# A hybrid RG-LRU and SSD layer on one core: seven weight subtractions, eight additions and the conv tails leave GpSimd, and the RG gate weights are issued first

## The chip, the cores and the metric

The kernel runs on one core of one Trainium2 chip. Its time is the device time of that core in microseconds. The matrix unit is called PE (weight loads: PEld), VectorE is DVE, ScalarE is ACT, GpSimd is POOL and SyncE is SP. PE shows two granted clocks in the records, 1.2 and 2.4 GHz, written 0.50 and 1.00; a stretch over which it changes shows a value between.

## The reference

One layer of a decoder trunk on T = 544 tokens: a prompt of 512 and eight samples of 4 tokens, width 1024, in fp32.

```
x = x + 0.5 * post1(SwiGLU1(pre1(x)))
x = x + postM(Mixer(preM(x)))
x = x + 0.5 * post2(SwiGLU2(pre2(x)))

proj = u @ w_in          # -> rg_x, rg_g, z, xbc, dt_raw, g_rg, g_ssd
rg_xc = causal_conv(rg_x)                     # 4 taps
gate_a = sigmoid(blockwise rg_xc @ wa + ba)   # 8 blocks of 128 x 128
gate_x = sigmoid(blockwise rg_xc @ wx + bx)
a = exp(-8 gate_a softplus(-lam));  h = scan(a, rg_xc gate_x sqrt(1 - a^2))
y_rg = h * gelu(rg_g)
xs, B, C = split(silu(causal_conv(xbc)))
y_ssd = rmsnorm_by_group((ssd_scan(xs, softplus(dt), A, B, C) + ssd_d * xs) * silu(z))
out = (sigmoid(g_rg) * (y_rg @ Wr) + sigmoid(g_ssd) * (y_ssd @ Ws)) @ w_out
```

It also returns the last state of both scans and the last three rows ahead of each convolution (the conv states), for the prompt and for every sample.

## The kernel before, in words

Activations lie transposed, features on the 128 partitions and the 544 tokens along the row, in two halves of 272. Every weight is fetched in raw tiles of up to 1024 x 256 by DMAs of SP (line 54; two tiles, so at most one is fetched ahead of the one in use). The class `Weights` cuts it into blocks of 1024 x 128 and splits each in two: ACT casts it to a high part `wh` (line 68), and a subtraction gives the low part `wl` (line 69). That subtraction is VectorE's, except in seven blocks, where the spec's flag `low` is set and the block's number is odd: there it is POOL's (line 61). Four blocks of `wh` and `wl` are kept, three of them ahead of use. A product is three matmuls for each 128 of depth and each half: high by high, low by high, high by low.

The work goes FFN1, mixer, FFN2. In the mixer, the first products (`first_products`, line 653) run dt and the first columns of the RG branch and fill tiles of the normalised activations; then come pairs of RG blocks, each with a background generator `rg_steps` (line 800): convolution (`conv`, four taps of VectorE at line 757), gate weights fetched and split (lines 806 to 812), gate products (line 830), the scan on VectorE (line 869) and the gelu product. Blocks (2, 3) and (0, 1) are first; a loop (line 1194) does (4, 5) and (6, 7). `dt_steps` (line 703) makes softplus, cumulated decays and their transposes (PE line 739) in the middle of that. Then eight SSD groups follow: convolution of B, C and x, chunked scan, gating, square (ACT line 1138), the sum of two squares (line 1141) and a matmul with ones (line 1146) for the group's norm. Behind them come the two output projections, the merge and FFN2.

`conv_last` (line 765) keeps the last three rows of each stretch of a convolution's input `cb` in a small tile `cq`, 9 stretches by 3 rows; it is called 40 times, with two POOL copies each time, the second after the first; PE transposes `cq` at line 776 for the conv states. `ssd_d` is fetched (lines 699 to 701) by two DMAs, each of 64 partitions by 16 elements that lie two elements apart in memory.

PE's order is written by hand (`tc.manual_schedule`, line 97): the products of the main path call `ptick` after each matmul, and every few matmuls one step of the oldest background generator is issued among them. The other engines' order is a scheduler's. POOL's DMAs share one queue (q0), SP's another (q1).

Of the kernel before, what the change touches and what calls it, by code (L numbers as in the profile page):

```python
# [9 lines left out]
F32 = mybir.dt.float32  # L10
# [8 lines left out]
P = 128  # L19
D = 1024  # L20
KD = 8
LP = 512
NB = 8
# [11 lines left out]
class Weights:  # L35
    def __init__(self, nc, pool, specs, ahead):
        self.nc = nc
        self.pool = pool
        self.specs = specs
        self.ahead = ahead  # L40
        self.blocks = [(s, o) for s, (ap, kt, cols, low) in enumerate(specs) for o in range(0, cols, P)]
        self.raw = {}
        self.done = {}
        self.n_raw = 0
        self.n_blk = 0
        self.pos = 0

    def _load(self):
        s = self.n_raw
        if s >= len(self.specs):  # L50
            return
        ap, kt, cols, low = self.specs[s]
        t = self.pool.tile([P, 8, 2 * P], F32, tag="wraw", name="wraw", bufs=WRAW)
        self.nc.sync.dma_start(t[:, :kt, :cols], ap.rearrange("(k p) c -> p k c", p=P))
        self.raw[s] = t
        self.n_raw += 1

    def _split(self):
        nc = self.nc
        s, o = self.blocks[self.n_blk]  # L60
        sub = nc.gpsimd if self.specs[s][3] and self.n_blk % 2 else nc.vector
        while self.n_raw <= min(s + WRAW - 1, len(self.specs) - 1):
            self._load()
        kt = self.specs[s][1]
        src = self.raw[s][:, :kt, o:o + P]
        h = self.pool.tile([P, 8, P], F32R, tag="wh", name="wh", bufs=WBLK)
        l = self.pool.tile([P, 8, P], F32R, tag="wl", name="wl", bufs=WBLK)
        nc.scalar.copy(h[:, :kt], src)  # L68
        sub.tensor_sub(l[:, :kt], src, h[:, :kt].bitcast(F32))  # L69
        self.done[self.n_blk] = (h, l)  # L70
        self.n_blk += 1

# [13 lines left out]
def hybrid_layer_kernel(  # L86
# [9 lines left out]
    nc = tc.nc  # L96
    ctx.enter_context(tc.manual_schedule(engines={mybir.EngineType.PE}))
    V, S, G, PE = nc.vector, nc.scalar, nc.gpsimd, nc.tensor
    dma = nc.gpsimd.dma_start
# [20 lines left out]
    FCH = (6, 8, 8)  # L120
    FC0 = (0, 6, 14)
# [5 lines left out]
    def end_order(kind, c):  # L127

        return [(kind, (c, n), 0) for n in range(4)] + [("post", 0, 0)] + [(kind, (c, n), 1) for n in SECOND] + [("post", 1, 1)]

    def ffn_order():

        order = [("gu", 0, 0), ("gu", 1, 0), ("gu", 1, 1), ("gu", 0, 1), ("gu", 2, None)]
        for c in range(3):
            if c:
                order += [("gu", p, None) for p in range(FC0[c] // 2 + 1, (FC0[c] + FCH[c]) // 2)]
            if c < 2:
                order += [("gu", FC0[c + 1] // 2, None)]
                order += [("wd", (c, n), None) for n in range(4)]
        return order + end_order("wd", 2)  # L140

    def ffn_specs(wg, wu, wd):
        sp = []
        for kind, i, h in ffn_order():
            if kind == "gu" and (i, h) != (1, 1):
                cs = slice(256 * i, 256 * i + 256)
                sp += [(wg[0, :, cs], 8, 256, False), (wu[0, :, cs], 8, 256, False)]
            elif kind == "wd" and not (h == 1 and i[1] in KEPT):
                c, n = i
                sp.append((wd[0, P * FC0[c]:P * (FC0[c] + FCH[c]), 256 * n:256 * n + 256], FCH[c], 256, False))  # L150
        return sp

    def win_spec(c0, n, low=False):
        return [(w_in[0, :, c0 + o:c0 + min(o + 256, n)], 8, min(256, n - o), low) for o in range(0, n, 256)]

    specs = ffn_specs(ffn1_wg, ffn1_wu, ffn1_wd)
    specs += win_spec(8192, 128)
# [5 lines left out]
    GATES_RG, GATES_SSD = ((0,), (1, 2), (3,)), ((), (4,), (), (5,), (), (6,), (), (7,))  # L163

    def gate_specs(qs):
        return [win_spec(8224 + 256 * q, 256, q < 3)[0] for q in qs]

    specs += gate_specs(GATES_RG[0])
    for i, r in enumerate(range(4, 8, 2)):
        specs += win_spec(128 * r, 256, True) + win_spec(1024 + 128 * r, 256, True) + gate_specs(GATES_RG[i + 1])  # L170
    for g in range(8):
        specs += win_spec(6144 + 128 * g, 128) + win_spec(7168 + 128 * g, 128) + win_spec(4096 + 256 * g, 256)
        a, b = gate_specs(GATES_SSD[g]), win_spec(2048 + 256 * g, 256)
        specs += b + a if g == 7 else a + b
    specs += [(w_proj_rg[0, :, 256 * q:256 * q + 256], 8, 256, False) for q in range(4)]
    for i in range(2):
        specs += [(w_proj_ssd[0, 1024 * i:1024 * i + 1024, 256 * q:256 * q + 256], 8, 256, False) for q in range(4)]
    for kind, i, h in end_order("out", 0):
        if kind == "out" and not (h == 1 and i[1] in KEPT):
            specs.append((w_out[0, :, 256 * i[1]:256 * i[1] + 256], 8, 256, False))  # L180
    specs += ffn_specs(ffn2_wg, ffn2_wu, ffn2_wd)
    W = Weights(nc, wpool, specs, WBLK - 1)

# [48 lines left out]
    def split(h, l, src):  # L232
        S.copy(h, src)
        V.tensor_sub(l, src, h.bitcast(F32))

    def wait(n):
        for _ in range(n):
            yield
# [432 lines left out]
    def mt(shape, tag, bufs, dt=F32):  # L671
        return pm.tile(shape, dt, tag=tag, name=tag, bufs=bufs)
# [7 lines left out]
    def t_b(shape, dt=F32):  # L680
        return mt(shape, "big", 12, dt)

    def t_s(shape, dt=F32):
        return mt(shape, "small", 14, dt)

    hfin = pm.tile([P, KD, 9], F32, name="hfin")
    tokT = pm.tile([P, 3, 4, 32], F32, name="tokT")
    toks = pm.tile([96, 3, 32], F32, name="toks")
    Es = pm.tile([P, 16, TS], F32, name="Es")
    Dc = pm.tile([P, 16], F32, name="Dc")  # L690
# [5 lines left out]
    dtc = pm.tile([32, 4], F32, name="dtc")  # L696
    dma(dtc[:, 0:1], ssd_dt_bias.rearrange("o h -> h o"))
    dma(dtc[:, 1:2], ssd_a_log.rearrange("o h -> h o"))
    for h2 in range(2):
        src = ssd_d.rearrange("o (q h) -> o h q", h=2)[0, h2:h2 + 1, :]  # L700
        dma(Dc[64 * h2:64 * h2 + 64, :], src.to_broadcast([64, 16]))

    def dt_steps(dt_):

# [48 lines left out]
    def conv(buf, ws, b):  # L753
        o = t_cv()
        S.activation(o[:, :CO], buf[:, 0:CO], AF.Identity, scale=ws[0], bias=b)  # L755
        for k in range(1, 4):
            V.scalar_tensor_tensor(o[:, :CO], buf[:, k:k + CO], ws[k], o[:, :CO], op0=ALU.mult, op1=ALU.add)  # L757
        ahead["cb"] -= 1
        return o
# [5 lines left out]
    def conv_last(buf):  # L765

        q = mt([P, 9, 3], "cq", 8)
        G.tensor_copy(q[:, 0:8], buf[:, LP:LP + 56].rearrange("p (b u) -> p b u", b=NB)[:, :, 0:3])
        G.tensor_copy(q[:, 8], buf[:, LP + 56:LP + 59])
        return q  # L770

    def conv_state(o_p, o_s, qs, f, df):
# [27 lines left out]
    def rg_steps(r0, bufs, gsb):  # L800
        qs = [lasts.pop(0) for _ in range(2)]
        rs = (r0, r0 + 1)
        col = lambda r, i: pT[:, r, i:i + 1]
        xcs, chs, wqs, gas, gxs, avs = [], [], [], [], [], []
        for r in rs:
            wr = t_s([P, 2, P])
            dma(wr[:, 0], rg_wa[0, r])
            dma(wr[:, 1], rg_wx[0, r])
            wq = [t_s([P, 2, P], F32R) for i in range(2)]
            split(wq[0], wq[1], wr)  # L810
            wqs.append(wq)
            xc = conv(bufs[r - r0], [col(r, R_RGW + i) for i in range(4)], col(r, R_RGB))
            ch = t_b([P, CB], F32R)
            cl = t_b([P, CB], F32R)
            split(ch[:, :CO], cl[:, :CO], xc[:, :CO])
            xcs.append(xc)
            chs.append((ch, cl))
            yield from wait(4)
# [95 lines left out]
    def group_steps(g, tiles):  # L914
# [73 lines left out]
        def fin():  # L988
            St = st8["S"]
            fs = ps_tile()  # L990
            for p in range(2):
                PE.transpose(fs[:, P * p:P * p + P], St[:, 2 * p:2 * p + 2].rearrange("p h d -> p (h d)"), ident)
            fo = t_s([P, 2, P])
            S.copy(fo, fs[:, :256].rearrange("p (a n) -> p a n", a=2))
            dma(o_p_ssd[0, 0, h4].rearrange("(a h) d n -> (h d) a n", a=2), fo)
# [133 lines left out]
        sqs = []  # L1129
        for p in range(2):  # L1130
# [6 lines left out]
            q = t_b([P, T])  # L1137
            S.activation(q, y, AF.Square, scale=0.5)
            ys.append(y)
            sqs.append(q)  # L1140
        G.tensor_add(sqs[0], sqs[0], sqs[1])
        fin()
        yield from wait(12)
        v = py_tile()
# [2 lines left out]
        r = sqs[1]  # L1147
# [11 lines left out]
    def rg_inputs(r):  # L1159
        bufs = []  # L1160
        for j in range(2):
            acc = unit(KD, xh, xl)
            bufs.append(rg_buf(r + j))
            for h in range(2):
                conv_in(bufs[j], acc[:, h, :TH], h)
        return bufs
# [25 lines left out]
    gate_units(GATES_RG[0])  # L1192
    bg.append(dt_steps(dt_))
    for i, r in enumerate(range(4, KD, 2)):
        b = rg_inputs(r)
        bg.append(rg_steps(r, b, rg_gates(r)))
        gate_units(GATES_RG[i + 1])
    for g in range(8):
        out = {}
        for i, f in enumerate((16 + g, 24 + g, 2 * g, 2 * g + 1)):  # L1200
            acc = unit(KD, xh, xl)
            q, t = f // 8, f % 8
            buf = conv_buf(cst[:, t, :].rearrange("p (b w q) -> p b w q", b=NB, w=3)[:, :, :, q])
# [64 lines left out]
    for n in range(KD):  # L1268
# [5 lines left out]
        h = mt([P, T], "mh", 8, F32R)  # L1274
        l = mt([P, T], "ml", 8, F32R)
# [98 lines left out]
```

## Time and profile before

| | |
|---|---|
| median of 3 runs | 1775.37 us (1774.06 to 1775.75) |
| profiled execution | 1772.28 us |
| its span | 1770.5 us |
| mean granted clock | 0.987 |
| PE busy | 1689.6 us (95%) |
| DVE busy | 1002.2 us (57%) |
| ACT busy | 730.4 us (41%) |
| POOL busy | 328.3 us (19%) |

The busy shares are averages over stages: FFN1 ends near 460 us of the span, the RG blocks lie between 460 and 680, the SSD groups between 680 and 1140, and projections and FFN2 fill the rest. PE is busy nearly always, so what can move the time is the sum of the short stretches in which PE waits, and those in which its granted clock is 0.50. POOL works only between about 440 and 1170 us.

### The profile page before, as it was taken

The numbers are of one execution on the slowest core, as the hardware profiler recorded it, in microseconds if no ns is written. First come the engines' busy times: TensorE is split into PE (matmuls) and PEld (weight loads), VectorE is DVE, ScalarE is ACT, GpSimd is POOL, SyncE is SP. The second block draws the span as 40 slices with busy tenths as digits, with TensorE's granted clock in tenths as the row PEclk, the third lists the DMA queues.
The fourth block names the chain that finished last, engine by engine and source line by source line (L and its number), as shares of the span: only waits on it lengthen the run. The fifth ranks groups of instructions, "written<-read, shape, count | busy, mean of one in ns | idle before, by whom it ended". The sixth has DMA issues, their size and how long they took to land. (4 is left out here: it accounts for less than half of the span.)

```text
span 1770.5 us, 31999 instructions
## 1 busy us (share of the span) xinstructions
PE 1689.6 (95%) x13419; PEld 1642.0 (93%) x13419; DVE 1002.2 (57%) x1728; ACT 730.4 (41%) x1145; POOL 328.3 (19%) x475
## 2 busy tenths in 40 slices
PE   7999999999989898998999999999999999999997
PEld 6999999999989897988988988899998999999996
DVE  5432333347556678788798687776557532233336
ACT  6322221234367585545445445433346323221232
POOL 0000000001143325355355445241000000000000
PEclk9999999999989899999999999999999999999998
DMA  6313323323742334433433544665424323223231
GB/s 199 108 54 114 96 72 96 96 96 104 113 147 91 113 107 123 143 114 102 142 116 113 149 127 131 204 192 192 176 95 138 100 69 119 81 87 96 85 107 51
DMA packets 204541, 206.17 MB, mean 116 GB/s; under 512 B 10493, under 2 KB 190777, under 8 KB 204142
## 3 DMA queue, kind: packets, MB, share of 16 engines
q1 hardware_dynamic: 196030, 179.61, 32.7%
q0 software_dynamic: 8368, 24.53, 5.0%
q8 instruction: 105, 1.72, 0.4%
q14 instruction: 38, 0.31, 0.1%
HBM read 178.42 MB, written 25.69 MB: 115 GB/s over the span
## 5 line engine op out<-in xcount | busy, mean ns | idle before, releaser
L68 ACT CAST wh<-wraw 128x1024 fp32r<-128x1024 f32 (+1 forms) x274 | 283.4, 1036 | 632.6 <-PE acc L268 519.0
L268 PE MATMUL acc<-xh,wh 128*128 128x272 f32 x2576 | 543.7, 292 | 0.0
L268 PE MATMUL acc<-xh,wl 128*128 128x272 f32 x2576 | 541.0, 291 | 0.0
L268 PE MATMUL acc<-xl,wh 128*128 128x272 f32 x2576 | 538.8, 290 | 0.0
L69 DVE TENSOR_TENSOR wl<-wraw,wh 128x1024 fp32r<-128x1024 f32 (+1 forms) x267 | 324.7, 1218 | 319.4 <-ACT wh L68 316.2
L268 PEld LDWEIGHTS acc<-xh,wh 128*128 128x128 f32 x2576 | 408.3, 190 | 3.6 <-issue 1.4
L268 PEld LDWEIGHTS acc<-xl,wh 128*128 128x128 f32 x2576 | 407.9, 190 | 1.2 <-issue 0.4
L268 PEld LDWEIGHTS acc<-xh,wl 128*128 128x128 f32 x2576 | 406.6, 190 | 2.2 <-issue 0.8
L300 PE MATMUL acc<-xh,wh 128*128 128x272 f32 x384 | 114.0, 297 | 1.5 <-DVE xl L518 1.5
L300 PE MATMUL acc<-xh,wl 128*128 128x272 f32 x384 | 113.5, 296 | 0.0
L300 PE MATMUL acc<-xl,wh 128*128 128x272 f32 x384 | 113.0, 294 | 0.0
L427 POOL TENSOR_TENSOR xT<-xT,rt 128x272 f32<-128x272 f32 x4 | 3.5, 886 | 534.4 <-DVE rt L426 534.4
L361 DVE TENSOR_TENSOR gate<-gate,acc 128x544 f32<-128x544 f32 x36 | 26.0, 722 | 132.0 <-PE acc L268 132.0
L757 DVE SCALAR_TENSOR_TENSOR cv<-cb,hp,cv 128x568 f32<-128x568 f32 x96 | 89.5, 932 | 6.0 <-ACT cv L755 4.9
L268 PE MATMUL acc<-hh,wh 128*128 128x272 f32 x448 | 92.5, 288 | 0.0
L268 PE MATMUL acc<-hl,wh 128*128 128x272 f32 x448 | 92.2, 287 | 0.0
L268 PE MATMUL acc<-hh,wl 128*128 128x272 f32 x448 | 92.1, 287 | 0.0
L628 POOL MEMSET cb<- 128x3 f32 x40 | 4.1, 102 | 471.3 <-PE acc L300 432.8
L300 PEld LDWEIGHTS acc<-xh,wh 128*128 128x128 f32 x384 | 73.9, 192 | 2.2 <-DVE xl L518 1.6
L300 PE MATMUL acc<-hh,wh 128*128 128x272 f32 x256 | 75.1, 293 | 0.0
L300 PEld LDWEIGHTS acc<-xl,wh 128*128 128x128 f32 x384 | 74.0, 193 | 0.5
L300 PEld LDWEIGHTS acc<-xh,wl 128*128 128x128 f32 x384 | 73.8, 192 | 0.4
(351 smaller groups left out, 2698.4 us busy)
## 6 DMA issues: line engine op xcount, KB each, us to landing
wraw<-in_w_in_dram SPq DMA_DIRECT2D x34, 1024.0 KB
wraw<-in_ffn_wg_dram SPq DMA_DIRECT2D x24, 1024.0 KB
wraw<-in_ffn_wu_dram SPq DMA_DIRECT2D x24, 1024.0 KB
wraw<-in_ffn_wd_dram SPq DMA_DIRECT2D x20, 1024.0 KB
wraw<-in_w_in_dram SPq DMA_DIRECT2D x18, 512.0 KB
big<-acs_dram SPq DMA_DIRECT2D x32, 256.0 KB
big<-in_state_ssd_dram SPq DMA_DIRECT2D x32, 256.0 KB
out_dram<-big POOLq DMA_DIRECT2D x32, 256.0 KB, 3.3
```

The source lines that it names most:

```text
L68: nc.scalar.copy(h[:, :kt], src)
L69: sub.tensor_sub(l[:, :kt], src, h[:, :kt].bitcast(F32))
L268: PE.matmul(acc[:, h, :TH], w[:, k, :], r[k][:, HALF[h]], start=(k == 0 and i == 0), stop=(k == kt - 1 and i == 2))
L300: PE.matmul(acc[:, j, :TH], w[:, k, :], r[k][:, HALF[h]], start=(k == 0 and i == 0), stop=(k == kt - 1 and i == 2))
L361: V.tensor_mul(two(gs[j]), two(gs[j]), acc[:, :, :TH])
L427: (G if shared and k % 2 else V).tensor_add(xT[:, k, cs], xT[:, k, cs], t)
L628: G.memset(buf[:, 0:3], 0.0)
L757: V.scalar_tensor_tensor(o[:, :CO], buf[:, k:k + CO], ws[k], o[:, :CO], op0=ALU.mult, op1=ALU.add)
```

## The change

Five edits, in one kernel:

- the flag `low` goes, and all 274 subtractions of `wl` are VectorE's;
- the RG gate weights are fetched by a function `rg_weights`: eight DMAs for blocks 2, 3, 0 and 1 as soon as the mixer's pools are open, ahead of the memsets of `cz` and the DMAs of `dtc`; the eight for blocks 4 to 7 at the start of the loop's two turns, ahead of their inputs;
- `ssd_d` is fetched as one contiguous row of 32 to every partition (`Dr`), and two VectorE copies pick the elements out;
- `conv_last` is one ACT copy with an access pattern written by hand, of nine stretches of 3 rows, 7 elements apart;
- the sum of two squares in a group is VectorE's.

```diff
@@ class Weights, _split
-        sub = nc.gpsimd if self.specs[s][3] and self.n_blk % 2 else nc.vector
...
         nc.scalar.copy(h[:, :kt], src)
-        sub.tensor_sub(l[:, :kt], src, h[:, :kt].bitcast(F32))
+        nc.vector.tensor_sub(l[:, :kt], src, h[:, :kt].bitcast(F32))
@@ mixer, where its pools open
+    def rg_weights(rs):
+
+        for r in rs:
+            wr = t_s([P, 2, P])
+            dma(wr[:, 0], rg_wa[0, r])
+            dma(wr[:, 1], rg_wx[0, r])
+            wrs[r] = wr
+
+    wrs = {}
+    rg_weights((2, 3, 0, 1))
...
+    Dr = t_s([P, 16, 2])
+    dma(Dr.rearrange("p q h -> p (q h)"), ssd_d.to_broadcast([P, 32]))
     for h2 in range(2):
-        src = ssd_d.rearrange("o (q h) -> o h q", h=2)[0, h2:h2 + 1, :]
-        dma(Dc[64 * h2:64 * h2 + 64, :], src.to_broadcast([64, 16]))
+        V.tensor_copy(Dc[64 * h2:64 * h2 + 64, :], Dr[64 * h2:64 * h2 + 64, :, h2])
@@ conv_last
         q = mt([P, 9, 3], "cq", 8)
-        G.tensor_copy(q[:, 0:8], buf[:, LP:LP + 56].rearrange("p (b u) -> p b u", b=NB)[:, :, 0:3])
-        G.tensor_copy(q[:, 8], buf[:, LP + 56:LP + 59])
+        a = buf[:, LP:LP + 1]
+        S.copy(q, bass.AP(a.tensor, a.offset, [list(a.ap[0]), [7, 9], [1, 3]]))
@@ rg_steps
-            wr = t_s([P, 2, P])
-            dma(wr[:, 0], rg_wa[0, r])
-            dma(wr[:, 1], rg_wx[0, r])
+            wr = wrs.pop(r)
@@ group_steps
-        G.tensor_add(sqs[0], sqs[0], sqs[1])
+        V.tensor_add(sqs[0], sqs[0], sqs[1])
@@ loop over r = 4, 6
+        rg_weights((r, r + 1))
         b = rg_inputs(r)
```

Line numbers after the change differ: the subtraction is line 68, the gate weights' DMAs lines 689 and 690, the scan 877, the conv taps 767, the sum of squares 1149. PE's order of instructions is the same in both kernels. POOL has 384 instructions in its order instead of 479, DVE 1311 rows instead of 1292, and ACT 40 more copies.

Where the mixer opens, POOL's order before, from the write of the residual to DRAM (`xs_dram`) to the first three pairs of gate weights:

```order
L603 DMA xs_dram_112<-xT_157 128x4352
L695 MEMSET cz0_4781 128x256
L695 MEMSET cz1_4782 128x256
L697 DMA dtc_4785<-in_ssd_dt_bias_dram 32x1
L698 DMA dtc_4785<-in_ssd_a_log_dram 32x1
L701 DMA Dc_4778<-in_ssd_d_dram 64x16x1 x2
L807 DMA small_5085<-in_rg_wa_dram 128x128
L808 DMA small_5085<-in_rg_wx_dram 128x128
L807 DMA small_5117<-in_rg_wa_dram 128x128
L808 DMA small_5117<-in_rg_wx_dram 128x128
L807 DMA small_5462<-in_rg_wa_dram 128x128
L808 DMA small_5462<-in_rg_wx_dram 128x128
```

The same place after the change, right behind the write of the residual:

```order
L689 DMA small_4774<-in_rg_wa_dram 128x128
L690 DMA small_4774<-in_rg_wx_dram 128x128
L689 DMA small_4777<-in_rg_wa_dram 128x128
L690 DMA small_4777<-in_rg_wx_dram 128x128
L689 DMA small_4780<-in_rg_wa_dram 128x128
L690 DMA small_4780<-in_rg_wx_dram 128x128
L689 DMA small_4783<-in_rg_wa_dram 128x128
L690 DMA small_4783<-in_rg_wx_dram 128x128
L704 MEMSET cz0_4793 128x256
L704 MEMSET cz1_4794 128x256
L706 DMA dtc_4797<-in_ssd_dt_bias_dram 32x1
L707 DMA dtc_4797<-in_ssd_a_log_dram 32x1
```

The gate weights stood behind the two memsets and four other DMAs, two of them those of `ssd_d`; now all eight of the first blocks stand ahead of them. The fetch of `ssd_d` is the next row, and the eight DMAs for blocks 4 to 7 follow it.

On VectorE, at the scans of the first pair of RG blocks (`big` and `in` are tiles of the RG steps, `cv` is a convolution's result, `cb` its input), the order before:

```order
L757 SCALAR_TENSOR_TENSOR cv<-cb,pT,cv 128x568 x2
L860 MEMSET in 128x1 x2
L757 SCALAR_TENSOR_TENSOR cv<-cb,pT,cv 128x568
L861 TENSOR_TENSOR in<-in 128x568 x2
L867 COPY in<-pT 128x8 x2
L869 SCALAR_TENSOR_TENSOR big<-big,in 128x568 x2
L870 COPY hfin<-big 128x9
L873 SCALAR_TENSOR_TENSOR big<-z,big 128x512
L874 SCALAR_TENSOR_TENSOR big<-z,big 128x32
```

and after, from the first scan to the second split of the next pair's convolution (line 233, which was line 234):

```order
L877 SCALAR_TENSOR_TENSOR big<-big,in 128x568
L875 COPY in<-pT 128x8
L68 TENSOR_TENSOR wl<-wraw,wh 128x1024
L878 COPY hfin<-big 128x9
L881 SCALAR_TENSOR_TENSOR big<-z,big 128x512
L882 SCALAR_TENSOR_TENSOR big<-z,big 128x32
L877 SCALAR_TENSOR_TENSOR big<-big,in 128x568
L788 COPY cs<-ps 27x256
L878 COPY hfin<-big 128x9
L881 SCALAR_TENSOR_TENSOR big<-z,big 128x512
L882 SCALAR_TENSOR_TENSOR big<-z,big 128x32
L233 TENSOR_TENSOR big<-cv,big 128x568
```

The three conv taps that stood ahead of the scans stand behind both splits of line 233 now; a weight subtraction that was POOL's stands between the scans, and the copy of `cs`, which was behind the first split of line 234, is ahead of it.

On VectorE in `dt_steps`, whose results PE transposes, the order before:

```order
L713 TENSOR_TENSOR big<-big 32x544
L714 SCALAR_TENSOR_TENSOR big<-big 32x544
L724 TENSOR_SCALAR big<-big,dtc 32x544
L744 COPY small<-big 32x96
L725 SCALAR_TENSOR_TENSOR big<-big 32x544
L730 TENSOR_TENSOR big<-big 32x512
L730 TENSOR_TENSOR big<-big 32x32
```

and after:

```order
L723 TENSOR_TENSOR big<-big 32x544
L724 SCALAR_TENSOR_TENSOR big<-big 32x544
L734 TENSOR_SCALAR big<-big,dtc 32x544
L754 COPY small<-big 32x96
L735 SCALAR_TENSOR_TENSOR big<-big 32x544
L68 TENSOR_TENSOR wl<-wraw,wh 128x1024
L740 TENSOR_TENSOR big<-big 32x512
L740 TENSOR_TENSOR big<-big 32x32
```

A weight subtraction has come between the second and the third result that PE transposes there.

## Rows read from the trace of the kernel before

**Rows 1.** Waits of PE: engine, line, waited for: us in total, times, longest.

```profile
PE py L300 <- ACT wh L68: 8.5, 1, 8.5
...
PE ps L776 <- POOL cq L769: 4.9, 1, 4.9
...
PE py L830 <- DVE big L234: 3.9, 2, 2.7
...
PE py L1146 <- POOL big L1141: 2.3, 1, 2.3
...
PE py L830 <- ACT in L832: 1.6, 1, 1.6
```

**Rows 2.** Windows: us, busy of PE, PEld, DVE, ACT, POOL, PEclk, DMA share, GB/s.

```profile
480.00:490.00 10.00, 3.79 (x31) 3.56 (x29) 0.00 (x0) 0.00 (x0) 0.00 (x0) 0.88 0.80 29
483.70:497.90 14.20, 5.31 (x22) 4.90 (x22) 6.10 (x8) 6.05 (x12) 2.68 (x4) 0.64 0.32 101
500.00:505.60 5.60, 5.60 (x47) 5.60 (x47) 5.09 (x8) 4.60 (x9) 1.13 (x4) 1.00 0.74 232
548.20:555.90 7.70, 4.97 (x27) 4.92 (x27) 7.19 (x14) 3.20 (x4) 2.44 (x6) 0.78 0.57 199
587.60:600.30 12.70, 8.13 (x43) 7.54 (x42) 10.67 (x19) 4.58 (x9) 4.17 (x9) 0.60 0.44 110
667.30:675.40 8.10, 3.25 (x16) 3.21 (x16) 6.69 (x14) 2.79 (x5) 7.22 (x8) 0.79 0.79 226
...
1137.30:1143.00 5.70, 3.36 (x11) 2.83 (x11) 2.40 (x3) 1.05 (x2) 2.35 (x1) 0.70 0.82 268
```

**Rows 3.** Timeline of ACT: start, us, instruction, idle before and its releaser.

```profile
490.84 0.40 ACT L233 CAST small<-small 128x256 fp32r<-128x256 f32 x1 [18.36 <-DMA small<-in_rg_wx_dram]
```

**Rows 4.** Timeline of POOL, the fetch of `ssd_d`.

```profile
467.22 1.67 POOL L701 DMA_DIRECT2D Dc<-in_ssd_d_dram  x2
```

**Rows 5.** Line 701's own view: landing of its two DMAs.

```profile
DMA to landing us min/median/max: 14.2/18.2/22.3
```

**Rows 6.** Line 698's own view: landing of `ssd_a_log`, issued just before.

```profile
DMA to landing us min/median/max: 3.6/3.6/3.6
```

**Rows 7.** Line 808's own view: its issues, and landing of eight DMAs of gate weights.

```profile
L808 POOL DMA_DIRECT2D small<-in_rg_wx_dram x8: 547/547/558, 469.5 to 610.3; - x8
...
DMA to landing us min/median/max: 2.1/3.9/21.3
```

**Rows 8.** Timeline of DVE, at the first scans and in `dt_steps`.

```profile
540.00 1.65 DVE L757 SCALAR_TENSOR_TENSOR cv<-cb,pT,cv 128x568 f32<-128x568 f32 x2
...
543.98 4.75 DVE L869 TENSOR_TENSOR_SCAN big<-big,in 128x568 f32<-128x568 f32 x2
...
585.67 2.73 DVE L713 TENSOR_TENSOR big<-big 32x544 f32<-32x544 f32 x1
...
635.18 1.33 DVE L869 TENSOR_TENSOR_SCAN big<-big,in 128x568 f32<-128x568 f32 x1
```

**Rows 9.** Timeline of POOL, at the same places, before group 0 and in a group.

```profile
543.87 2.43 POOL L69 TENSOR_TENSOR wl<-wraw,wh 128x1024 fp32r<-128x1024 f32 x1
...
584.92 2.90 POOL L69 TENSOR_TENSOR wl<-wraw,wh 128x1024 fp32r<-128x1024 f32 x1
...
666.36 5.64 POOL L768 COPY cq<-cb 128x24 f32<-128x24 f32 x1
...
1136.84 2.81 POOL L1141 TENSOR_TENSOR big<-big 128x544 f32<-128x544 f32 x1 [5.58 <-ACT big L1138]
```

**Rows 10.** Groups of instructions: count, busy us, mean ns, idle before and releaser.

```profile
L69 DVE TENSOR_TENSOR wl<-wraw,wh 128x1024 fp32r<-128x1024 f32 (+1 forms) x267 | 324.7, 1218 | 319.4 <-ACT wh L68 316.2
...
L1135 DVE TENSOR_TENSOR big<-big,z 128x544 f32<-128x544 f32 x16 | 11.6, 724 | 0.4
```

**Rows 11.** Windows, columns as in rows 2: ahead of group 0, and group 0 on.

```profile
671.90:683.40 11.50, 11.21 (x78) 11.21 (x79) 6.62 (x12) 4.72 (x7) 3.09 (x11) 0.85 0.57 170
683.00:783.00 100.00, 95.32 (x810) 89.70 (x809) 83.34 (x176) 49.40 (x94) 48.45 (x73) 1.00 0.41 118
```

More of the change, by code (lines that the diff above doesn't have):

```diff
@@ L40, in __init__ @@
         self.ahead = ahead
-        self.blocks = [(s, o) for s, (ap, kt, cols, low) in enumerate(specs) for o in range(0, cols, P)]
+        self.blocks = [(s, o) for s, (ap, kt, cols) in enumerate(specs) for o in range(0, cols, P)]
         self.raw = {}
@@ L51, in _load @@
             return
-        ap, kt, cols, low = self.specs[s]
+        ap, kt, cols = self.specs[s]
         t = self.pool.tile([P, 8, 2 * P], F32, tag="wraw", name="wraw", bufs=WRAW)
@@ L146, in ffn_specs, with win_spec @@
                 cs = slice(256 * i, 256 * i + 256)
-                sp += [(wg[0, :, cs], 8, 256, False), (wu[0, :, cs], 8, 256, False)]
+                sp += [(wg[0, :, cs], 8, 256), (wu[0, :, cs], 8, 256)]
             elif kind == "wd" and not (h == 1 and i[1] in KEPT):
                 c, n = i
-                sp.append((wd[0, P * FC0[c]:P * (FC0[c] + FCH[c]), 256 * n:256 * n + 256], FCH[c], 256, False))
+                sp.append((wd[0, P * FC0[c]:P * (FC0[c] + FCH[c]), 256 * n:256 * n + 256], FCH[c], 256))
         return sp
-    def win_spec(c0, n, low=False):
-        return [(w_in[0, :, c0 + o:c0 + min(o + 256, n)], 8, min(256, n - o), low) for o in range(0, n, 256)]
+    def win_spec(c0, n):
+        return [(w_in[0, :, c0 + o:c0 + min(o + 256, n)], 8, min(256, n - o)) for o in range(0, n, 256)]
     specs = ffn_specs(ffn1_wg, ffn1_wu, ffn1_wd)
@@ L165, in gate_specs @@
     def gate_specs(qs):
-        return [win_spec(8224 + 256 * q, 256, q < 3)[0] for q in qs]
+        return [win_spec(8224 + 256 * q, 256)[0] for q in qs]
     specs += gate_specs(GATES_RG[0])
     for i, r in enumerate(range(4, 8, 2)):
-        specs += win_spec(128 * r, 256, True) + win_spec(1024 + 128 * r, 256, True) + gate_specs(GATES_RG[i + 1])
+        specs += win_spec(128 * r, 256) + win_spec(1024 + 128 * r, 256) + gate_specs(GATES_RG[i + 1])
     for g in range(8):
@@ L174, in hybrid_layer_kernel @@
         specs += b + a if g == 7 else a + b
-    specs += [(w_proj_rg[0, :, 256 * q:256 * q + 256], 8, 256, False) for q in range(4)]
+    specs += [(w_proj_rg[0, :, 256 * q:256 * q + 256], 8, 256) for q in range(4)]
     for i in range(2):
-        specs += [(w_proj_ssd[0, 1024 * i:1024 * i + 1024, 256 * q:256 * q + 256], 8, 256, False) for q in range(4)]
+        specs += [(w_proj_ssd[0, 1024 * i:1024 * i + 1024, 256 * q:256 * q + 256], 8, 256) for q in range(4)]
     for kind, i, h in end_order("out", 0):
         if kind == "out" and not (h == 1 and i[1] in KEPT):
-            specs.append((w_out[0, :, 256 * i[1]:256 * i[1] + 256], 8, 256, False))
+            specs.append((w_out[0, :, 256 * i[1]:256 * i[1] + 256], 8, 256))
     specs += ffn_specs(ffn2_wg, ffn2_wu, ffn2_wd)
```

## The prediction

> **What bounds the kernel now.** PE does, apart from short stretches. I read first PE's waits [rows 1]: the reader is to see that the five lines listed name engines that this change touches, 8.5 us behind a weight cast of ScalarE, 4.9 behind POOL's copies, 2.7 behind VectorE's split, 2.3 behind POOL's addition, 1.6 behind ScalarE. Then windows around each [rows 2]: a wait is followed by a stretch at a granted clock of 0.50, so it costs more than it lasts. The row from 500.00 is the yardstick: 47 matmuls in 5.6 us at clock 1.00, 8.4 a us. What a window lost is its length less its matmuls over 8.4. From 483.7: 14.2 - 22/8.4 = 11.6 us (place A). From 548.2: 7.7 - 27/8.4 = 4.5 (B). From 587.6: 12.7 - 43/8.4 = 7.6 (C, the transposes of `dt_steps`). From 667.3: 8.1 - 16/8.4 = 6.2 (F). From 1137.3: 5.7 - 11/8.4 = 4.4 (H). With the wait of 1.6 on ScalarE (D, at the gate products of the later blocks) they hold 35.9 us of the profiled execution of 1772.3. Last I read what released each, on its own engine.
>
> **A, the first gate weights: 11.6.** ScalarE sat 18.36 us at the cast of gate weights that a DMA had not brought, until 490.84 [rows 3]; the weight cast that PE needed stands behind it in ScalarE's order. That DMA was queued behind the two of `ssd_d`, issued from 467.22 [rows 4], which landed after 14.2 and 22.3 us [rows 5], while the small one issued just ahead of them took 3.6 [rows 6]. In the ten us from 480 the DMA engines were 0.80 busy and moved 29 GB/s, while VectorE and ScalarE did nothing [rows 2]: the queue was slow by the shape of what it moved. The Trainium skill, "DMA: Bandwidth & Descriptors", "Rules for kernel authors", says that a last dimension with a stride becomes one descriptor per element; 2 x 64 x 16 elements would be 2048 of them. The busy share beside the low rate agrees with it; by that rule the new `Dr`, a contiguous run per partition, is quick, and by the other reading (weights waiting for bandwidth) rival 1 would come.
>
> After the change eight gate-weight DMAs stand first, behind the write of the residual only. POOL came to the fetch of `ssd_d` at 467.2 [rows 4] after two memsets and two issues; I estimate from that that it got past the residual's write and its wait for VectorE near 465.5, and take the same start here, as the gate weights' tile lies in memory that is freed then. Eight issues of 0.55 [rows 7] end at 470, and at 2.1 to 3.9 us a landing [rows 7] the last is there near 474, 17 us before it was. ScalarE then casts them when it comes to them, and the weight cast behind is early. The whole 11.6 goes, clock included, since PE has no wait left there. What is late next: the memsets of `cz` and the DMAs of `dtc` start 4.4 us later; ScalarE waits for `dtc` in place of the gate weights, to 475 by the 3.6 of rows 6, where PE has products until 483.7. That is hidden; without the cover it would cost those 4.4.
>
> **D: 1.6.** The weights of the last blocks were issued as late as 610.3 [rows 7], and ScalarE waited for them ahead of the activation that PE wanted. They now follow the first eight on POOL, more than 100 us sooner, and the wait goes.
>
> **B, the first scans: 4.1.** PE waited 2.7 us for VectorE's split at line 234. By the order three conv taps now stand behind it, 3 x 0.82 = 2.5 [rows 8]. The two scans took 4.75 where one takes 1.33 elsewhere [rows 8], and POOL's subtraction ran beside them [rows 9]: 4.75 - 2.66 = 2.1 that goes with POOL's part. Against that stand the subtraction now on VectorE, 1.2 [rows 10], and the copy of `cs`, 256 elements wide, for which I take the 0.4 of ScalarE's cast of as many [rows 3]. In sum 3.0 earlier, against 2.7: the wait mostly goes, and I take 2.3 of it and the 1.8 of clock. The margin is thin; its bounds are 0 and 4.5.
>
> **C: 0.9 of 7.6.** POOL's subtraction ran from 584.92 to 587.82 [rows 9], beside VectorE's line 713, which took 2.73 [rows 8] where a 128x544 operation takes 0.72 [rows 10]: 2.0 goes. But the subtraction of 1.2 now stands between the second and the third result, so the first two waits shorten and the third stays. I take 0.9 and no clock, bounds -1.2 and 7.6.
>
> **F, the conv tails: 5.1.** POOL's first copy took 5.64 us before group 0 [rows 9]. On ScalarE it is a copy of 27 elements, and 256 took 0.40 there [rows 3]; I estimate half of that. The wait and its clock, 6.2, go. But PE comes to group 0 that much earlier and finds VectorE with its work still to do: between 671.9 and 683.4 VectorE was idle for 11.5 - 6.6 = 4.9 us [rows 11], and what PE gains beyond that is given back, 6.2 - 4.9 = 1.3, of which I count 1.1. Forty such copies cost ScalarE 40 x 0.2 = 8 us; upper bound the 0.40, 16. ScalarE is half idle in the groups (49 of 100 busy, [rows 11]), so this lies beside other work, save where PE waits for ScalarE.
>
> **H, the sum of squares: 2.2.** POOL's addition took 2.81 there [rows 9], VectorE's takes 0.72 [rows 10], but a subtraction of 1.2 stands ahead of it, of which I take 0.9 to be left when the square is done. 2.8 - 0.7 - 0.9 = 1.2 less wait, and half of the 4.4 - 2.3 = 2.1 of clock: 2.2.
>
> **The groups: -2.** VectorE gets eight additions of 0.72, 5.8 us, where it is 83 of 100 busy [rows 11], and in four of the groups the addition stands right behind the product that ScalarE squares, so that VectorE waits for the square, at most another 0.72 each by the nearest row. Behind it there are the decay products that PE wants next. The upper bound is 8 x 1.44 = 11.5, the lower 0 (or a gain, where POOL no longer disturbs VectorE). PE has products queued for much of it; I take 2.
>
> **The other moved subtractions** (those of the seven that are not in B and C) cost VectorE 5 x 1.2 = 6.1 between 460 and 680; in the ten us from 480 VectorE does nothing at all, and one that is late shows only if the block is wanted within its own length, with three blocks ahead. I count nothing; without this cover, 6.1.
>
> Sum: 11.6 + 1.6 + 4.1 + 0.9 + 5.1 + 2.2 - 2.0 = 23.5. The profiled execution would take 1772.3 - 23.5 = 1748.8. The median of the runs lies 3.1 us above the profiled one (1775.4 against 1772.3), so the forecast is 1751.9.
>
> **Rivals.**
> 1. *The gate weights still land late*, because something other than `ssd_d` fills the DMA engines. Raw weight tiles and the write of the residual go over the same engines at that time; if their landing took 15 us instead of 4, ScalarE would be held till 485 and A would give 11.6 - 7 = 4.6. Against it: the DMA just before took 3.6 [rows 6]. Sum 16.5, time 1758.9. 4 in 100.
> 2. *The early gains are given back in the groups.* PE reaches group 0 about 22 us sooner than before, VectorE is 83 of 100 busy there, B and C stay, and the groups take 6 instead of 2. Then 11.6 + 1.6 + 5.1 + 2.2 - 6.0 = 14.5 are left: 1760.9. What speaks for it is that VectorE's work ahead of group 0 was hidden beside the waits; against it, the 4.9 us in which it idled just ahead of group 0 [rows 11]. 20 in 100.
> 3. *Slower: the additions make VectorE the bound.* VectorE is in order; in every group its decay products wait behind the addition and that behind ScalarE's square: 1.44 each, and PE waits long enough for the clock to fall, 2.1 as at H. Eight times 3.5 is 28.3, against 25.5 of gains: 1778.2. It decides from 25.5/8 = 3.2 us a group. Against it: the 1.44 must not be hidden in any group, while PE was 95 of 100 busy at clock 1.00 [rows 11]. 3 in 100.
> 4. *More than forecast.* POOL has disturbed VectorE in more places than the two I priced: the scans at 4.75 and line 713 at 2.73 are such. If C goes whole, and the groups lose nothing, the sum is 23.5 + 6.7 + 2.0 = 32.2: 1743.2. The Trainium skill, "SBUF — State Buffer", "Who interferes with whom", has a rule for this: an operation of VectorE with two inputs in SBUF and one of GpSimd that reads SBUF exclude each other, and the second to issue waits for the whole of the first. The scans and line 713 agree with it. By it the change helps more, since POOL's reads mostly go, but a moved subtraction can itself stand behind one of POOL's remaining products; no row here shows that. 13 in 100.
>
> **How the numbers follow.** The forecast has 60 in 100, with 1747 to 1757 as its own range. The range of 8 in 10 takes in B and C at their bounds and most of rivals 1, 2 and 4: 1742 to 1764. Less than 0.2% (3.6 us), about what a measurement of this kernel can tell, counts as no change. Rivals 1, 2 and 4 are faster all the same; with half of rival 3 and what I overlook, slower 0.03, same 0.04, faster 0.93.
>
> **What would show it.** In the profile after: ScalarE's wait at the gate cast near 472 is under 5 us, and PE has no wait over 1 us at 492 and no low clock there. If it still waits, and the gate DMAs land after over 10 us, rival 1. PE's wait at line 776 before group 0 is gone or under 1 us. The two scans take under 3 us. At the transposes of `dt_steps` PE still waits, mostly at the third result. In the groups the waits of PE on VectorE and ScalarE grow by 2 us or so in sum; over 6, rival 2, and over 25 with low clock in most groups, rival 3. The prediction is wrong if the time is above 1764 or A's 11.6 us are not gone.

## The result and the profile after

The changed kernel takes 1746.7 us (median of 4, 1746.0 to 1747.0) against 1775.5 (median of 4, 1774.1 to 1775.8): the ratio is 0.9838, 95% interval 0.9824 to 0.9852, 28.8 us faster. The forecast was 1751.9, and its range 1742 to 1764.

The head of the page after, to set beside the table of before: POOL worked 64 us less, VectorE 0.7 less though it does the work of seven subtractions and eight additions more, ScalarE 5 more.

```profile
span 1745.3 us, 31942 instructions
...
PE 1683.0 (96%) x13419; PEld 1636.6 (94%) x13419; DVE 1001.5 (57%) x1745; ACT 735.2 (42%) x1185; POOL 264.7 (15%) x379
```

PE's waits after (engine, line, waited for: us in total, times, longest), those that answer to [rows 1]; the waits at lines 299 on the weight cast, 786 (the tails' transposes) and on ScalarE at 838 are gone. Of line 838's two waits for VectorE, the one at the first scans is 0.2.

```profile
PE ps L749 <- DVE big L743: 2.8, 1, 2.8
...
PE ps L944 <- DVE in L911: 1.4, 1, 1.4
PE py L1154 <- DVE big L1149: 1.4, 1, 1.4
PE py L838 <- DVE big L233: 1.3, 2, 1.1
```

Windows after, columns as in [rows 2]: the place of the first gate weights, of the first scans, of `dt_steps`, and of the norm's matmul. The same 14.2 us that held 22 matmuls hold 115 now, at clock 1.00. At `dt_steps` alone the clock still falls (0.76).

```profile
483.70:497.90 14.20, 14.20 (x115) 14.20 (x115) 10.92 (x13) 9.89 (x18) 2.05 (x4) 1.00 0.56 165
534.00:540.60 6.60, 6.40 (x50) 6.17 (x49) 6.60 (x13) 3.50 (x5) 2.18 (x4) 1.00 0.74 247
571.00:585.00 14.00, 9.87 (x60) 9.33 (x59) 11.56 (x22) 5.78 (x14) 0.52 (x1) 0.76 0.33 81
...
1112.00:1118.30 6.30, 4.94 (x36) 4.57 (x36) 3.87 (x7) 4.71 (x6) 0.48 (x2) 1.00 0.51 152
```

Landing of the gate weights (line 690, eight DMAs; [rows 7] had a longest of 21.3), and then of `ssd_d` (line 709; 14.2 and 22.3 in [rows 5]):

```profile
DMA to landing us min/median/max: 2.2/3.4/5.2
```

```profile
DMA to landing us min/median/max: 3.1/3.1/3.1
```

VectorE at the first scans after, to set beside [rows 8]: 1.33 each, with the moved subtraction between them.

```profile
530.83 1.33 DVE L877 TENSOR_TENSOR_SCAN big<-big,in 128x568 f32<-128x568 f32 x1
532.08 0.15 DVE L875 COPY in<-pT 128x8 f32<-128x8 f32 x1
532.14 1.22 DVE L68 TENSOR_TENSOR wl<-wraw,wh 128x1024 fp32r<-128x1024 f32 x1
...
534.05 1.33 DVE L877 TENSOR_TENSOR_SCAN big<-big,in 128x568 f32<-128x568 f32 x1
```

The two moved groups that were priced (count, busy us, mean ns, idle before and its releaser): the 40 tails on ScalarE at 0.225 us each, and the eight additions on VectorE at 0.722, before which VectorE waited 2.9 us in all for the squares.

```profile
L779 ACT COPY cq<-cb 128x27 f32<-128x27 f32 x40 | 9.0, 225 | 0.5
...
L1149 DVE TENSOR_TENSOR big<-big 128x544 f32<-128x544 f32 x8 | 5.8, 722 | 2.9 <-ACT big L1146 2.9
```

PE has the same order of matmuls in both kernels and in all variants but two, so the n-th matmul of one timeline can be set against the n-th of the other; the difference of their starts is what has been saved up to there. Worked out so from the profiled executions, in us, for the forecast, the changed kernel and the first four experiments (row: `ssd_d` alone; order: gate weights first alone; tails: conv tails alone; subs: subtractions alone):

| place | forecast | after | row | order | tails | subs |
|---|---|---|---|---|---|---|
| A, first gate weights | 11.6 | 11.7 | 11.7 | -1.4 | -1.8 | 0.3 |
| B, first scans | 4.1 | 4.1 | 0.3 | 0.1 | 2.6 | -0.4 |
| C, `dt_steps` | 0.9 | 0.9 | 0.7 | 0.4 | 0.1 | 0.9 |
| D, later gate products | 1.6 | 1.9 | -0.3 | 1.9 | 1.9 | 0.0 |
| F, tails, to group 0 | 5.1 | 4.9 | -1.0 | -0.6 | 4.9 | -0.1 |
| groups, up to H's wait | -2.0 | 0.4 | -1.6 | -1.7 | -0.6 | 0.0 |
| H, the wait at the norm's matmul and its clock | 2.2 | 2.5 | 2.0 | 1.8 | 1.3 | -0.1 |

The starts of the last matmuls lie 25.9 us apart in the changed kernel; what the table leaves of it (-0.6) lies ahead of A and behind H. Each column is one execution: C comes out at 1.4 in two later variants that don't touch it, so differences of half a microsecond say nothing. Groups and H hang together: there a fall of the clock comes at one wait or at another, 1.5 us or so each time, and a gain of 2.0 at H beside a loss of 1.6 in the groups, as in the run with `ssd_d` alone, is no gain.

### The profile page after: what moved, and what is told of

Read it like the earlier page. It is cut to its first block, busy times and chain, and to the rows that moved or that the text cites. A ratio compares the mean times of both kernels' runs of the same rounds, so it can differ in the third digit from the quotient of the medians.

```text
span 1745.3 us, 31942 instructions
## 1 busy us (share of the span) xinstructions
PE 1683.0 (96%) x13419; PEld 1636.6 (94%) x13419; DVE 1001.5 (57%) x1745; ACT 735.2 (42%) x1185; POOL 264.7 (15%) x379
## 5 line engine op out<-in xcount | busy, mean ns | idle before, releaser
L68 DVE TENSOR_TENSOR wl<-wraw,wh 128x1024 fp32r<-128x1024 f32 (+1 forms) x274 | 333.2, 1217 | 323.5 <-ACT wh L67 320.3
L360 DVE TENSOR_TENSOR gate<-gate,acc 128x544 f32<-128x544 f32 x36 | 25.9, 721 | 132.0 <-PE acc L267 132.0
```

The source lines that it names most:

```text
L68: nc.vector.tensor_sub(l[:, :kt], src, h[:, :kt].bitcast(F32))
L360: V.tensor_mul(two(gs[j]), two(gs[j]), acc[:, :, :TH])
```

## The experiments

The theory was that each place is bought by its own edit, and A by what the two DMAs of `ssd_d` did to the queue behind them. The first four do one edit alone on the kernel before.

**`ssd_d` as one row, alone.**

```diff
+    Dr = t_s([P, 16, 2])
+    dma(Dr.rearrange("p q h -> p (q h)"), ssd_d.to_broadcast([P, 32]))
     for h2 in range(2):
-        src = ssd_d.rearrange("o (q h) -> o h q", h=2)[0, h2:h2 + 1, :]
-        dma(Dc[64 * h2:64 * h2 + 64, :], src.to_broadcast([64, 16]))
+        V.tensor_copy(Dc[64 * h2:64 * h2 + 64, :], Dr[64 * h2:64 * h2 + 64, :, h2])
```

> Only ssd_d is fetched as one contiguous row and copied; the gate weights keep their late place in POOL's order. Theory (the shape of the two ssd_d DMAs blocks the queue): the gate weights land within 4 us, PE's wait of 8.5 us on the cast goes with its low clock, 11.6 us saved at that place; the wait of 1.6 at the later blocks' gate products stays, B, C, F, H stay: 1764 us (before at 1775.5). Rival (the weights are late by their place in the order, behind memsets and four DMAs, or by bandwidth): 0 to 4 us saved, 1772 to 1775.

1763.9 us, ratio 0.9941 (0.9926 to 0.9955). A gave its whole 11.7 with the gate weights at their old, late place: of the eight DMAs of line 809, none landed later than 5.3 us, and PE's waits at the other places stayed.

```profile
DMA to landing us min/median/max: 2.0/4.2/5.3
```

```profile
PE ps L777 <- POOL cq L770: 4.9, 1, 4.9
PE py L831 <- DVE big L234: 3.9, 2, 2.7
PE py L831 <- ACT in L833: 1.9, 1, 1.9
```

**The gate weights first, alone.**

```diff
+    wrs = {}
+    rg_weights((2, 3, 0, 1))
...
-            wr = t_s([P, 2, P])
-            dma(wr[:, 0], rg_wa[0, r])
-            dma(wr[:, 1], rg_wx[0, r])
+            wr = wrs.pop(r)
...
+        rg_weights((r, r + 1))
         b = rg_inputs(r)
```

> Only the order of the gate weights' DMAs is changed; ssd_d keeps its two strided DMAs, now behind the first eight. Theory (a queue is held by what stands ahead in it): 11.6 us at the first gate weights and 1.8 at the later blocks' gate products are saved, 13.4 in sum: 1762 us. Rival (the strided DMAs keep the 16 DMA engines busy for everybody, raw weight tiles too): PE then waits for a weight block whose raw tile is late, at least 4 of the 13.4 stay: 1766 or more.

1771.8 us, ratio 0.9988 (0.9979 to 0.9997): the theory failed here and the rival held. The 2.1 us by the medians are about what D gave (1.9); A lost 1.4. The first eight gate weights had landed by 476.0 us, and PE then waited longer than before, at another instruction. PE's longest wait in this kernel, and ScalarE's timeline (the copy that PE waited for stands behind the second cast there):

```profile
PE acc L300 <- ACT z L662: 10.3, 1, 10.3
```

```profile
482.30 1.05 ACT L68 CAST wh<-wraw 128x1024 fp32r<-128x1024 f32 x1
502.89 1.04 ACT L68 CAST wh<-wraw 128x1024 fp32r<-128x1024 f32 x1 [19.54 <-DMA wraw<-in_w_in_dram]
```

ScalarE waited 19.54 us for a raw weight tile, which is another queue's. SP had issued the fetch of one at 479.44:

```profile
479.44 0.37 SPq L54 DMA_DIRECT2D wraw<-in_w_in_dram  x1
```

The windows show why it was late: for ten us the DMA engines were 0.89 busy and moved nothing that shows in GB/s (last column), while PE still ran on what it had. All packets of these ten us are of POOL's queue (rows in the last section).

```profile
480.00:490.00 10.00, 10.00 (x83) 10.00 (x82) 6.08 (x7) 3.36 (x8) 0.54 (x1) 1.00 0.89 0
490.00:500.00 10.00, 4.28 (x35) 4.07 (x33) 0.00 (x0) 0.00 (x0) 1.15 (x7) 0.82 0.45 154
```

So the strided fetch does not only hold what is behind it in its queue; it holds the engines that all queues share, for some 20 us, and who is held up is a matter of who is asking then. In the kernel before it was the gate weights; SP issued no weight tile there between 466.67 and 493.47.

**The conv tails on ScalarE, alone.**

```diff
-        G.tensor_copy(q[:, 0:8], buf[:, LP:LP + 56].rearrange("p (b u) -> p b u", b=NB)[:, :, 0:3])
-        G.tensor_copy(q[:, 8], buf[:, LP + 56:LP + 59])
+        a = buf[:, LP:LP + 1]
+        S.copy(q, bass.AP(a.tensor, a.offset, [list(a.ap[0]), [7, 9], [1, 3]]))
```

> Only the conv tails go from POOL to ScalarE. Theory: 6.5 us are saved at the transposes of the tails ahead of group 0, 1.5 of them given back there, and in the order two or three conv taps of VectorE now stand behind the first scans, so that up to 4 us at the wait of 2.7 are saved as well by the order alone, though POOL's subtraction still runs beside the scans; the groups gain 1 us for 80 POOL reads fewer. In sum 9 us: 1766.5. Rival (the 4.1 us at the first scans came from POOL's subtraction that stopped disturbing them): nothing is saved at the scans, sum 5 to 6: 1770.

1762.8 us, ratio 0.9935 (0.9918 to 0.9951): 11 by the medians, 8.9 by the profiled executions. F is 4.9, and 2.6 at the first scans came with POOL's subtraction still beside them: the conv taps left their place ahead of the scans. That subtraction is seen in VectorE's timeline there: a copy of eight elements took 2.31, until POOL's subtraction ended at 546.57; in the changed kernel the same copy took 0.15.

```profile
543.04 1.33 DVE L869 TENSOR_TENSOR_SCAN big<-big,in 128x568 f32<-128x568 f32 x1
544.29 2.31 DVE L867 COPY in<-pT 128x8 f32<-128x8 f32 x1
```

```profile
543.48 3.09 POOL L69 TENSOR_TENSOR wl<-wraw,wh 128x1024 fp32r<-128x1024 f32 x1 [12.05 <-ACT wh L68]
```

D's 1.9 came as well, which I had given to the order of the gate weights alone. In POOL's timeline of before, a pair of them stood behind a tail that waited for ScalarE (`cb`, line 640):

```profile
605.72 0.32 POOL L768 COPY cq<-cb 128x24 f32<-128x24 f32 x1 [4.73 <-ACT cb L640]
605.98 0.38 POOL L769 COPY cq<-cb 128x3 f32<-128x3 f32 x1
606.31 0.55 POOL L807 DMA_DIRECT2D small<-in_rg_wa_dram  x1
606.84 0.55 POOL L808 DMA_DIRECT2D small<-in_rg_wx_dram  x1
```

The landing 4.1 us later is the 610.96 at which ScalarE's cast started. Without tails on POOL the same pair went out 6.7 us earlier, while PE came there only 1.8 earlier:

```profile
599.64 0.55 POOL L807 DMA_DIRECT2D small<-in_rg_wa_dram  x1 [0.24 <-issue]
600.17 0.55 POOL L808 DMA_DIRECT2D small<-in_rg_wx_dram  x1
```

**The subtractions on VectorE, alone.**

```diff
-        sub = nc.gpsimd if self.specs[s][3] and self.n_blk % 2 else nc.vector
+        sub = nc.vector
```

> Only the seven subtractions go from POOL to VectorE. Theory: the scans fall from 4.75 to 2.7 us, but the subtraction of 1.2 stands ahead of the split PE waits for and the conv taps stay ahead of the scans, so 0 to 1.5 us are saved at the first scans; 0.9 at the transposes of dt_steps; sum 1 to 2: 1774. Rival (contention was the whole cause at the first scans): 4.1 saved there: 1770.5. Rival (VectorE gets late everywhere): slower by 3 or more: 1778.5.

1773.9 us, ratio 0.9996 (0.9986 to 1.0005): nothing. C gave 0.9; at B the scans fell to 1.33 and 1.32, but two subtractions and the copy of `cs` stood among them and the three conv taps ahead, and PE waited 3.1 instead of 2.7.

The next runs take an edit out of the changed kernel, or leave only two in.

**The strided fetch back in the changed kernel.**

```diff
-    Dr = t_s([P, 16, 2])
-    dma(Dr.rearrange("p q h -> p (q h)"), ssd_d.to_broadcast([P, 32]))
     for h2 in range(2):
-        V.tensor_copy(Dc[64 * h2:64 * h2 + 64, :], Dr[64 * h2:64 * h2 + 64, :, h2])
+        src = ssd_d.rearrange("o (q h) -> o h q", h=2)[0, h2:h2 + 1, :]
+        dma(Dc[64 * h2:64 * h2 + 64, :], src.to_broadcast([64, 16]))
```

> The changed kernel with ssd_d fetched by its two strided DMAs again, behind the first eight gate-weight DMAs. Theory, after the run with the order alone (the strided DMAs hold the DMA engines for everybody, so the raw weight tiles of SP's queue stop too): PE waits some 10 us for a raw tile at about 500 us and has a low clock behind it, 11 to 13 us slower than the changed kernel: 1758 to 1760 (changed kernel at 1746.7). Rival (the order protects what PE needs, and the run with the order alone was late for another reason): 1747 to 1749.

1758.1 us (1756.6 to 1759.0): 11.3 slower than the changed kernel, as the order-alone run said. PE's wait is the same one, 10.2 us, and the engines are 0.90 busy at 1 GB/s.

```profile
PE acc L299 <- ACT z L661: 10.2, 1, 10.2
```

```profile
480.00:490.00 10.00, 10.00 (x82) 10.00 (x81) 4.92 (x6) 1.92 (x4) 0.54 (x1) 1.00 0.90 1
```

**The gate weights at their old place in the changed kernel.**

```diff
-            wr = wrs.pop(r)
+            wr = t_s([P, 2, P])
+            dma(wr[:, 0], rg_wa[0, r])
+            dma(wr[:, 1], rg_wx[0, r])
```

> The changed kernel with the gate weights fetched in rg_steps again, as before. Theory, after the single runs (the fetch of ssd_d was what was late, and the tails' copies on POOL were what stood ahead of the later blocks' weights): PE has no wait of over 1 us at 492 or 595, the time is that of the changed kernel, 1746 to 1748. Rival (the order is worth its 1.9 at the later blocks' gate products): that wait is back, 1749.

1745.4 us (1744.6 to 1746.5), ratio 0.9832 (0.9817 to 0.9847): not slower. With `ssd_d` as a row and the tails off POOL, the order of the gate weights is worth nothing.

**Only `ssd_d` and the tails.** The two diffs of the first and the third run, on the kernel before.

> Only two edits of the five: ssd_d as one row, and the conv tails on ScalarE. Theory (these two are the change; the order of the gate weights is worth nothing beside them, the subtractions and the additions 1 to 3 us each): 11.5 + 9 saved, 1753 by the sum of the single runs, between 1748 and 1753. Rival (the order of the gate weights is needed for the wait at the later blocks' gate products, 1.9): that wait of over 1.5 us is still there and the time is 1755 or more.

1750.8 us (1747.7 to 1752.7), ratio 0.9868 (0.9847 to 0.9888): 24 of the 28.8 us. PE waits 1.7 at the first scans, nothing at the later gate products, and 2.6 for POOL's addition.

**The subtractions back on POOL in the changed kernel.** The line of the fourth run, the other way.

> The changed kernel with the seven subtractions on POOL again. Theory (in the order of this kernel the conv taps partly leave the path of the first scans, and POOL's subtraction beside the scans costs VectorE 2 there and 2 beside the third line of dt_steps): PE waits again at the first scans, 1 to 3 us with clock, and 0.9 more at the transposes of dt_steps: 1749 to 1751. Rival (the subtractions are worth nothing, as alone on the kernel before): 1747. Rival (VectorE gets its 8.5 us back): 1744.

1745.7 us (1744.9 to 1747.0), ratio 0.9841 (0.9824 to 0.9859). B moved as expected, 1.4 lost; `dt_steps`, where 0.9 more was to be lost, won 1.3: the subtraction no longer stands ahead of the third result, and PE waits 3.3 us there in all instead of 4.1. So the time is the rival's, that of the changed kernel.

```profile
PE py L839 <- DVE big L234: 2.7, 2, 1.6
PE ps L750 <- DVE big L744: 1.8, 1, 1.8
PE ps L750 <- DVE big L736: 1.5, 1, 1.5
```

**The addition back on POOL in the changed kernel.**

```diff
-        V.tensor_add(sqs[0], sqs[0], sqs[1])
+        G.tensor_add(sqs[0], sqs[0], sqs[1])
```

> The changed kernel with the sum of two squares on POOL again. Theory (the addition on POOL makes PE wait 1.0 to 1.2 longer ahead of the norm's matmul of group 6, and the longer wait brings the low clock with it, 1.6): 1747.5 to 1750. Rival (VectorE is relieved of 5.8 us in the groups, where it is the busiest engine after PE): 1744 to 1746.

1750.2 us (1748.3 to 1752.9), ratio 0.9857 (0.9837 to 0.9876): 3.5 slower than the changed kernel by the medians, 5.1 by the profiled executions. The run with the gate weights at their old place, timed beside it, took 1744.6 to 1746.5, so this one is slower than the like of it too. PE waits 2.7 instead of 1.4, and the clock falls behind it, in the window behind the wait to 0.79 (it was 1.00):

```profile
PE py L1154 <- POOL big L1149: 2.7, 1, 2.7
```

```profile
1115.00:1123.00 8.00, 5.26 (x26) 4.72 (x26) 3.73 (x5) 3.73 (x5) 2.81 (x1) 0.79 0.75 228
```

3.0 of the 5.1 are lost there, 1.4 in the wait and 1.6 in the clock behind it; 2.0 are lost earlier in the groups, most of it where the clock is at 0.50 from 880.4 to 887.2, twice as long as at the same place in the changed kernel. The run with only `ssd_d` and the tails, whose addition is POOL's too, has the same 6.8 us there; the cause I did not find.

**The wait that the change left.** In the changed kernel PE waits 2.8 us for the third result of `dt_steps`, with low clock behind it. Two kernels put the transposes 8 background steps later (a background step is one piece of other work that PE's order sets between the matmuls of the main path); the second also takes out the 8 steps behind them.

```diff
         V.tensor_mul(t2, t2, dt_)
-        yield from wait(16)
+        yield from wait(24)
```

> The changed kernel with the transposes of dt_steps put 8 background steps later in PE's order. Theory (the last place of the five that the change left: PE waits 2.85 us for VectorE's third result and then 6.8 us at the low clock, 6 us in sum): the wait goes and nothing needs the transposes sooner, 5 to 6 us faster than the changed kernel: 1741. Rival (what comes behind is pushed back by 32 matmuls and meets group 0, or the clock falls anyway): 1745 to 1748.

1747.4 us (1746.4 to 1748.6): no gain. C gave 7.1 instead of 0.9, and all of it was gone at group 0: PE waited there twice for VectorE instead of once 1.4, and VectorE had been busy 19.75 of 20 us ahead of it. The second window is the changed kernel's: VectorE is as full there, with PE still at work. That VectorE's unfinished work is what takes the gain back is my reading of these rows; the next run bears it out in part.

```profile
PE ps L944 <- DVE in L911: 7.5, 2, 3.9
```

```profile
640.00:660.00 20.00, 13.88 (x111) 13.46 (x109) 19.75 (x38) 12.86 (x20) 7.10 (x12) 0.97 0.60 180
...
640.00:660.00 20.00, 19.61 (x158) 19.32 (x156) 19.97 (x40) 16.02 (x29) 5.96 (x12) 1.00 0.55 162
```

```diff
-        yield from wait(8)
-        S.activation(Es, Es, AF.Exp)
+
+    def es_steps():
+        S.activation(Es, Es, AF.Exp)
+        yield
...
         bg.append(rg_steps(r, b, rg_gates(r)))
+        if i == 0:
+            bg.append(es_steps())
```

> The changed kernel with the transposes of dt_steps 8 background steps later, as in the run before, but the 8 steps that followed them taken out (the exponential of the samples' decays follows the next blocks' steps), so that nothing behind is issued later than in the changed kernel. Theory (the 6 us were given back because every later step on VectorE was pushed back by 8 background steps and VectorE is full from 640 to 680): now they stay in part, 3 to 6 us faster than the changed kernel: 1741 to 1744. Rival (whatever PE gains ahead of group 0 VectorE takes back there): 1745 to 1747, with PE's wait at line 944 grown to over 5 us.

1743.3 us (1743.0 to 1744.9), ratio to the kernel before 0.9822 (0.9807 to 0.9836): the fastest. Each of its runs lies below each of the changed kernel's, by medians 3.4. But the two were not timed side by side, and the intervals of their ratios overlap, so that the size of the gain is not sure; the places are of one execution each. Of the 6 us at `dt_steps` 4.6 more came than in the changed kernel, 2.1 of them went again at group 0, where one wait is left,

```profile
PE ps L946 <- DVE in L913: 3.8, 1, 3.8
```

and the groups behind it took 1.3 less: the clock did not fall where it falls at 881 us in the changed kernel.

## Why the prediction came out as it did

The time fell within the range and on the side forecast. By its steps:

- *A, 11.6.* The size was right (11.7), and the shape of `ssd_d`'s DMAs was named as what was slow. But the step gave the gain to the gate weights' place in POOL's queue as well ("eight gate-weight DMAs stand first"), and this half failed: the order alone saved nothing there (-1.4), the row alone saved it all (11.7). That the size came out is due to the row, and the change would have lost nothing at A without the new order. What I had not asked was who else uses the engines that were 0.80 busy: raw weight tiles do, and with the gate weights out of the way it was they that came 20 us late. Rival 1 looked for a second cause of lateness in the weights' own landing; the second victim was the right question.
- *D, 1.6.* Right in size (1.9), by the wrong edit: a tail's copy that waited for ScalarE held the DMAs behind it on POOL. Either edit alone removes it; neither adds to the other.
- *B, 4.1.* Right, and its two causes are separable: 2.6 comes with the tails alone, through the place of the conv taps, and the rest only when the subtractions are VectorE's too. The subtractions alone lost 0.4. The thin margin held.
- *C, 0.9.* The size is as worked out. The first two waits shrank (0.5 is left at the second); the third, which was to stay, grew from 1.6 to 2.8.
- *F, 5.1.* 6.5 saved and 1.5 given back at group 0, where PE waits 1.4 for VectorE at line 944: 4.9.
- *H and the groups, 2.2 and -2.0.* The wait fell from 2.3 to 1.4 (1.2 less was forecast, 1.0 came), and the clock did not fall behind it (1.6, where half of 2.1 was counted). The term of the groups was wrong: they gained 0.4 instead of losing 2.0. By the table's caution the two are best read together: forecast 0.2, measured 2.9 in the changed kernel and -2.1 with the addition back on POOL. VectorE's additions took the 5.8 us that were priced and 2.9 of waiting, all beside other work, and the run with the addition back on POOL was slower, not faster. Rival 3 needed 3.2 us a group; it had none.
- *The offset.* I added 3.1 us for the distance of before's profiled execution from its median; the changed kernel's profiled execution lay 0.3 above its own. Of the error of 5.2 us, 3.4 is this step, and the other 1.8 is the term of the groups above all. The executions of the kernel before, in the later comparisons, spread over 1770.7 to 1779.5, so the place of one of them against the median is chance; the four of the changed kernel lay within 1746.0 to 1747.0, which is too few to say whether it spreads less. I did not test what spreads them.

Rival 2 (gains given back where VectorE is full) was wrong in size for this change: 1.5 us were given back at group 0. As a mechanism it came in the run with the transposes later, which gave back all of its 6 us there.

## What to carry to other kernels

When a small DMA is slow, look at the busy share of the DMA engines beside their rate: where they are busy and move nothing, as here, the transfers of the other queue wait too, and issuing the one that is late earlier only changed the victim; mend the shape of the slow one. An in-order engine that both computes and issues DMAs (POOL here) delays its DMAs by what its copies wait for. And a wait that is taken away ahead of a stretch where another engine is full pays only if that engine's work isn't pushed back by it: take out as many steps behind as you put in ahead.

## What the runs showed of the hardware

Two DMAs of 64 x 16 single elements, 8 KB in sum, kept the 16 DMA engines about 0.9 busy for the whole of 480 to 490 us in two kernels, at 0 and 1 GB/s, and landed after 13 to 23 us; all packets that the DMA view of the run with the order alone shows there are of POOL's queue (its rows: packets and MB of all queues; then queue, packets, MB, share of 16 engines):

```profile
DMA packets 32, 0.00 MB, mean 0 GB/s; under 512 B 32, under 2 KB 32, under 8 KB 32
...
q0 software_dynamic: 32, 0.00, 89.2%
```

Half of these 32 are of 4 bytes and short. In the kernel before, the packet records have the 8 KB as 32 packets of 256 bytes, 64 elements each, with a median of 8.44 us. From 471.5 to 472.7 six of them start there, and nothing else (a packet counts whole where it starts): 2.637 x 16 x 1.2 / 6 = 8.4 us of one engine each.

```profile
DMA packets 6, 0.00 MB, mean 1 GB/s; under 512 B 6, under 2 KB 6, under 8 KB 6
...
q0 software_dynamic: 6, 0.00, 263.7%
```

By an estimate from these records that is 0.13 us an element, and 32 x 8.4 / 16 = 17 us of all 16 engines.

The Trainium skill, "DMA: Bandwidth & Descriptors", "Rules for kernel authors", has the shape (one descriptor per element of a strided last dimension), and the gain from the contiguous row, 22.3 to 3.1 us a landing, agrees with it.

A copy of eight elements on VectorE took 2.31 us beside a POOL subtraction, 0.15 without. The Trainium skill, "SBUF — State Buffer", "Who interferes with whom", says that copies can take the port pair that VectorE shares with GpSimd and that the second to issue then waits for the whole of the first; the row agrees, as the copy ends when the subtraction does (546.60 and 546.57).
